# The transposes of w_up's result behind later products, and the first unit's sums of u one stage earlier

## The chip, the cores and the metric

One core of one Trainium2 chip runs the whole kernel. The metric is the device time of one execution in microseconds (us). Three runs of the kernel before took 1495.15, 1499.13 and 1501.15 us; their median, 1499.13 us, stands for it.

## The reference, cut to what matters

One decoder layer on 256 tokens of width 2048: a mixer (state-space heads and attention heads from one projection `w_in`, joined by `w_out`), added to h, and then an MLP, added to h as well. The change lies in the MLP:

```python
def squared_relu_mlp(u, w_up, w_down):
    hdn = jax.nn.relu(jnp.einsum('bsd,df->bsf', u, w_up))
    return jnp.einsum('bsf,fd->bsd', hdn * hdn, w_down)

h = h + rmsnorm(squared_relu_mlp(rmsnorm(h, norm_mlp_pre), w_up, w_down), norm_mlp_post)
```

`w_up` is 2048 x 8192 and `w_down` 8192 x 2048, all in float32.

## The kernel before, in words

**Products.** Every float32 operand is split into a high and a low part of a faster type, `hi` by ScalarE (ACT, L137) and `lo` by VectorE (DVE, L138, which needs `hi`). A product is then three matmuls, lines 249 to 251 (or 331 to 333). Weights come by DMA in tiles `raw` of two slices of 128 rows (a *pair*), 512 columns wide; `raw` has four buffers, `hi` and `lo` five. So ACT's `hi` of a tile waits until TensorE (PE) is done with the tile five before it.

**Units.** `unit` computes two neighbouring blocks of 512 columns at once, for both tiles of 128 tokens, in four accumulators `acc` (PSUM banks). In w_up it has eight pairs. Pairs 2, 4 and 5 are *sevens*: the 2x2x2 block products of such a pair are done with seven multiplications in place of eight, from sums of weight blocks (L212 on DVE) and sums of activation blocks (`sums_of_acts`: L289 to L292 on DVE, then a split into `ha`). Four of the seven products go to four more banks, `more`, which `combine_new` adds in after the last seven. From one unit to the next `acc` and `more` change places. The sums of activations are made in the first unit that needs them and used by all units of that half.

**The end of a w_up unit.** Pairs 6 and 7 come last, first for block 0, then for block 1. When a block's token tile is complete, `up_end` makes a tile `r` or `junk` of it: an add on DVE (L1145) and two activations, relu and square (L1146, L1147). Then `turned` transposes it on PE with four 128x128 transposes (L1156) into the bank that the accumulator had, and splits it into `sh`/`sl` or `ah`/`al`, which are w_down's activations. A unit thus leaves four such *turns*: 1 and 2 for block 0 (token tiles 0 and 1), 3 and 4 for block 1. Their banks are, in the next unit, `more[0]`, `more[2]`, `more[1]` and `more[3]`. There is one buffer `junk` (turns 1 and 3) and there are two buffers `r` (turns 2 and 4, and also the temporary tiles of sums and sevens).

**What sets the order.** Code is recorded in program order, and a scheduler that estimates times then orders each engine's queue; each engine runs its queue in that order. `tc.high_priority` moves an operation ahead of all others that are ready by that estimate; `tc.issue_after(x)` keeps it behind x. Turns are generators in the queue `waiting`: `pump` advances one of them after each pair's products of one block; `drain` runs all to the end, and each unit does that ahead of its first seven. A turn needs two steps: the first does nothing, the second records transposes and splits.

**The stages around the change.** After the mixer and the first rows of w_up, `gemm_features` does one block of w_up with the weights as the stationary operand (L366, L369): the *feature block*. Then come three w_up units (blocks 2 to 7), two w_down units, four w_up units of the second half, and two last w_down units. While the feature block runs, h, which lies in the tiles `ha` and `hb`, goes to DRAM (`copies`, L1134), for the sums of u in the first unit are put in its place. Before the last two units h comes back the same way.

Of the kernel before, what the change touches and what calls it, by code (L numbers as in the profile page):

```python
# [16 lines left out]
P = 128  # L17
S = 256
D = 2048
NT = S // P  # L20
# [28 lines left out]
SUMS = 10  # L49
FINE = 4  # L50
FIRST = 3


def constants():
# [18 lines left out]
def hymba_layer(ctx: ExitStack, tc: tile.TileContext, x, norm_mix_pre, w_in, conv_w, conv_b, dt_bias, a_log,  # L73
                d_skip, ssm_norm_w, w_out, norm_mix_post, norm_mlp_pre, w_up, w_down, norm_mlp_post,
                consts, out):
    nc = tc.nc
    w_in, w_out, w_up, w_down = w_in[0], w_out[0], w_up[0], w_down[0]
# [30 lines left out]
    def part(k):  # L108
        return (sh, sl, k) if k < NK else (att["h"], att["l"], k - NK)
# [3 lines left out]
    ident = cst[:, 0:P]  # L113
# [8 lines left out]
    def bank():  # L122
        return pacc.tile([P, NB], F32, name="acc")

    def psmall():
        return psm.tile([P, NB], F32, name="ps")
# [7 lines left out]
    def split(hi, lo, src, scale=None):  # L134

        if scale is None:
            return (nc.scalar.activation(hi, src, AF.Copy),  # L137
                    nc.vector.tensor_tensor(lo, src, hi.bitcast(F32), op=ALU.subtract))  # L138
        return (nc.scalar.activation(hi, src, AF.Copy, scale=scale),  # L139
                nc.vector.scalar_tensor_tensor(lo, src, scale, hi.bitcast(F32), op0=ALU.mult, op1=ALU.subtract))  # L140
# [21 lines left out]
    def in_place_of_h(acts):  # L162

        a = hp.tile([P, 3 * KB, 2, S], F32R, name="ha")
        room["sums"] = [a[:, k] for k in range(3 * KB)]
        if acts is part:
            b = hp.tile([P, KB, 2, S], F32R, name="hb")
            room["sums"] += [b[:, k] for k in range(KB)]
            room["sums"] += [hp.tile([P, 2, S], F32R, name="wpost", bufs=2) for _ in range(2)]
        else:  # L170
            b = hp.tile([P, NT, NB], F32, name="hb")
            room["shared"] = [[b[:, t] for t in range(NT)],
                              [hp.tile([P, NB], F32, name="wpost", bufs=2) for _ in range(NT)]]
        room["raw"] = None
        room["acts"] = acts
        sums_of.clear()
# [13 lines left out]
    product = {}  # L190
# [39 lines left out]
    waiting = deque()  # L230

    def pump(n=1):
        for _ in range(n):
            if waiting:
                work = waiting.popleft()
                if next(work, work) is not work:
                    waiting.append(work)

    def drain():
        while waiting:  # L240
            pump()
# [11 lines left out]
    def row_tiles(src, c0, ks, acc, acts, first=True, last=True, lag=0, at_end=None, pumps=1, fetch=fetch):  # L253


        held = {}
        n = len(ks)
        for i in range(n + lag):
            if i < n:
                held[i] = weights(src, ks[i] * KB, c0, fetch)  # L260
            for t, at in ((0, i), (1, i - lag)):
                if not 0 <= at < n:
                    continue
                row_tile(acc[t], t, held[at], ks[at], acts, first and at == 0, last and at == n - 1)
                if at == n - 1 and at_end:
                    at_end(t, acc[t])
            pump(pumps)

    def gemm_tokens(src, c0, acts, nk, lag=0, at_end=None, pumps=1):

        acc = [bank() for _ in range(NT)]
        row_tiles(src, c0, range(nk // KB), acc, acts, True, True, lag, at_end, pumps)
        return acc
# [6 lines left out]
    def sums_of_acts(k):  # L280

        if k in sums_of:
            return sums_of[k]
        places = room["sums"][2 * len(sums_of):][:2]
        h_, l_, r = room["acts"](k * KB)
        with tc.high_priority(offset=AHEAD):
            a, c = (tmp().rearrange("p (i s) -> p i s", s=P) for _ in range(2))
            ah_, al_ = (v[:, r:r + KB].bitcast(F32).rearrange("p j (t s) -> p j t s", t=NT) for v in (h_, l_))
            nc.vector.tensor_tensor(a.rearrange("p (j t) s -> p j t s", t=NT), ah_, al_, op=ALU.add)  # L289
            nc.vector.tensor_tensor(c[:, 0:2], a[:, 0::3], a[:, 1:2].to_broadcast([P, 2, P]), op=ALU.subtract)  # L290
            nc.vector.tensor_tensor(c[:, 2], a[:, 0], c[:, 1], op=ALU.add)
            nc.vector.tensor_tensor(c[:, 3], a[:, 2], c[:, 2], op=ALU.subtract)  # L292
            ch, cl = (v.rearrange("p b (t s) -> p (b t) s", t=NT) for v in places)
            split(ch, cl, c)
        sums_of[k] = ch, cl
        return ch, cl
# [38 lines left out]
    def unit(src, n, order, last, acc, more, combine, lag=0, at_end=(None, None), first=True, ending=None):  # L335


        cols = (n * NB, (n + 1) * NB)
        sevens = [k for k, by_seven in order if by_seven]
        for i, (k, by_seven) in enumerate(order):  # L340
            if i + 1 < len(order) and order[i + 1][1]:
                sums_of_acts(order[i + 1][0])
            if by_seven:
                if k == sevens[0]:
                    drain()
                seven(src, *cols, k, acc, more, k == sevens[0], k == sevens[-1])
            else:
                for b in range(2):
                    row_tiles(src, cols[b], [k], acc[b::2], room["acts"], first and i == 0, False,
                              fetch=fetch_next)  # L350
            if k == sevens[-1]:
                combine(more)
        for b in range(2):
            if b and ending:
                ended.append(ending(cols[b], last, acc))
            else:
                row_tiles(src, cols[b], last, acc[b::2], room["acts"], False, True, lag if b else 0, at_end[b],
                          fetch=fetch if b else fetch_next)
# [258 lines left out]
    def first_conv(dst, ft0):  # L617

        for _ in range(FIRST):
            yield  # L620
# [157 lines left out]
    for hb in range(4):  # L778
# [10 lines left out]
        acc = gemm_tokens(w_in, COL_V + hb * NB, act_u, NK)  # L789
# [25 lines left out]
    def tmp():  # L815
        return hp.tile([P, NB], F32, name="r", bufs=2)

    def columns(n):
        return slice(n * NB, (n + 1) * NB)

    def in_mw(n):
        return [[mw[:, t, columns(n + b)] for t in range(NT)] for b in range(2)]
# [197 lines left out]
    acc = [bank() for _ in range(2 * NT)]  # L1020
# [31 lines left out]
    more = [psmall(), bank(), psmall(), bank()]  # L1052
# [7 lines left out]
    def order_of(ks, by_seven):  # L1060
        return [(k, k in by_seven) for k in ks]
# [5 lines left out]
    acc, more = more, acc  # L1067
# [55 lines left out]
    def onto(n):  # L1123

        def at_end(t, acc):
            m = mw[:, t, columns(n)]
            nc.vector.tensor_tensor(m, acc, m, op=ALU.subtract if n % 2 else ALU.add)
        return at_end

    def copies(dst, src):  # L1130

        for t in range(NT):
            for n in range(4):
                nc.scalar.dma_start(dst(t, columns(n)), src(t, columns(n)))  # L1134
                yield

    def in_dram(t, cs):
        return h_d[:, t, cs]
# [12 lines left out]
    def turned(t, k, r, p):  # L1151
        yield
        ts = slice(t * P, (t + 1) * P)
        with tc.high_priority(offset=AHEAD):
            for f in range(4):
                nc.tensor.transpose(p[:, f * P:(f + 1) * P], r[:, f * P:(f + 1) * P], ident)  # L1156
            d_h, d_l, i = part(k)
            split(d_h[:, i:i + 4, ts], d_l[:, i:i + 4, ts], p.rearrange("p (f s) -> p f s", f=4))

    waiting.append(copies(in_dram, of_h))  # L1160
    acc = gemm_features(w_up, NB, begun)
    for b in range(2):
        r = hp.tile([P, 2, S], F32, name="r", bufs=2)
# [3 lines left out]
    drain()  # L1167
    acc, more = [bank() for _ in range(2 * NT)], [psmall(), bank(), psmall(), bank()]
    for hf in range(2):
        in_place_of_h(act_u)  # L1170
        for fb in range(0 if hf else 2, 8, 2):
            unit(w_up[:, hf * 4096:], fb, order_of(range(6), (2, 4, 5)), (6, 7), acc, more,
                 lambda x: combine_new(room["shared"], x), 0, (up_end(fb, 0), up_end(fb + 1, 1)))
            acc, more = more, acc
        if hf == 0:
            drain()
            in_place_of_h(part)
            unit(w_down, 0, order_of(range(14), (4, 6, 9, 11, 13)), (14, 15), acc, more,
                 lambda x: combine_new(in_mw(0), x), 0, (onto(0), onto(1)))
            unit(w_down, 2, order_of((0, 1, 4, 2, 6, 3, 9, 5, 11, 7, 13, 8), (4, 6, 9, 11, 13)), (10, 12, 14, 15), more, acc,  # L1180
                 lambda x: combine_new(in_mw(2), x), 0, (onto(2), onto(3)))
    drain()
    new_h()
    waiting.append(copies(of_h, in_dram))

    def complete(n):
        def at_end(t, acc):
# [41 lines left out]
```

## Time and profile before

| what | us |
|---|---|
| runs (median of three) | 1499.13 |
| the profiled execution's own time | 1494.39 |
| its span, from first to last instruction | 1492.6 |
| PE busy in the span | 1469.8 |
| DVE busy in the span | 1192.9 |
| ACT busy in the span | 847.2 |

Times of single instructions come from the profiled execution, in us from the start of its span; its own time is 1.8 us longer than the span. A matmul of 512 columns is shown as 0.39 us long, but the next one starts 0.23 us after it, since they are pipelined; so a stretch of PE work is measured here from start to start. "Idle before" is the time in which an engine's queue stood still before an instruction, with what released it.

### The profile page before, as it was taken

How to read it: one execution, taken by the hardware profiler on the slowest of the kernel's cores; microseconds unless marked ns; L12 is line 12 of the kernel's file. 1: busy time of each engine (PE TensorE's matmuls, PEld its weight loads, DVE VectorE, ACT ScalarE, POOL GpSimd, SP SyncE). 2: the span in 40 equal slices, each digit the busy share in tenths (PEclk: the TensorE clock that was granted, in tenths of full speed). 3: DMA queues.
4: the chain of work that ended last, by engine and by line, in shares of the span. 5: the costliest groups of instructions: out<-in, count | busy, mean ns of one | idle time of the engine just before them, and what ended most of it. 6: DMA issues, size and time to landing. Idle time of an engine off the chain costs nothing.

```text
span 1492.6 us, 19937 instructions
## 1 busy us (share of the span) xinstructions
PE 1469.8 (98%) x7240; PEld 1235.7 (83%) x7240; DVE 1192.9 (80%) x1764; ACT 847.2 (57%) x1165; POOL 48.7 (3%) x67
## 2 busy tenths in 40 slices
PE   9999999999999999999999999999999999999998
PEld 8888888888888888888878777788888777878886
DVE  6798797886555555588988888889887898889998
ACT  7475675455545454555557566655554665565553
POOL 0003200220000000000000000000000000000000
PEclk9999999999999999999999999999999999999999
DMA  7665666555655555576557466645665666576663
GB/s 268 204 206 177 183 184 193 175 169 169 182 166 175 170 172 180 192 245 204 197 192 228 139 197 192 204 169 192 212 222 176 186 208 197 165 264 211 211 211 113
DMA packets 151283, 287.32 MB, mean 192 GB/s; under 512 B 11680, under 2 KB 14608, under 8 KB 151184
## 3 DMA queue, kind: packets, MB, share of 16 engines
q1 hardware_dynamic: 143456, 272.50, 58.2%
q10 hardware_dynamic: 7728, 13.54, 2.8%
q8 instruction: 57, 0.93, 0.2%
q14 instruction: 42, 0.34, 0.1%
HBM read 281.78 MB, written 4.23 MB: 192 GB/s over the span
## 4 chain that ended last, share of the span: by engine, by line
PE 88%; DVE 5%; ACT 3%; DMA 2%; issue 1%; SPq 0%; POOL 0%; POOLq 0%; ACTq 0%; DVEq 0%
PE acc L366 17%; PE acc L251 12%; PE acc L249 12%; PE acc L250 12%; PE acc L369 8%; PE acc L331 3%; PE acc L332 3%; PE acc L333 3%; PE ps L249 2%; PE ps L250 2%; PE ps L251 2%; DVE lo L138 2%; ACT hi L137 1%; PE ps L333 1%; PE ps L332 1%
## 5 line engine op out<-in xcount | busy, mean ns | idle before, releaser
L138 DVE TENSOR_TENSOR lo<-raw,hi 128x1024 fp32r<-128x1024 f32 (+1 forms) x476 | 580.9, 1224 | 209.8 <-ACT hi L137 203.6
L137 ACT ACTIVATE hi<-raw 128x1024 fp32r<-128x1024 f32 (+1 forms) x476 | 498.7, 1054 | 414.1 <-PE acc L251 131.2
L366 PE MATMUL acc<-ua,hi 128*128 128x512 f32 x680 | 186.9, 404 | 0.5 <-DVE ua L140 0.5
L366 PEld LDWEIGHTS acc<-ua,hi 128*128 128x128 f32 x680 | 120.2, 189 | 19.7 <-DVE ua L140 0.7
L249 PE MATMUL acc<-hi,ua 128*128 128x512 f32 x312 | 122.7, 393 | 0.0
L251 PE MATMUL acc<-hi,ua 128*128 128x512 f32 x312 | 122.2, 392 | 0.0
L250 PE MATMUL acc<-lo,ua 128*128 128x512 f32 x312 | 122.1, 391 | 0.0
L369 PEld LDWEIGHTS acc<-ua,lo 128*128 128x128 f32 x680 | 99.9, 189 | 11.7
L369 PE MATMUL acc<-ua,lo 128*128 128x256 f32 x680 | 103.1, 281 | 0.0
L137 ACT ACTIVATE hi<-e 128x1024 fp32r<-128x1024 f32 x51 | 54.1, 1062 | 61.9 <-DVE e L212 55.9
L249 PE MATMUL acc<-hi,sh 128*128 128x512 f32 x224 | 88.3, 394 | 0.0
L251 PE MATMUL acc<-hi,sl 128*128 128x512 f32 x224 | 87.4, 390 | 0.0
L250 PE MATMUL acc<-lo,sh 128*128 128x512 f32 x224 | 87.3, 390 | 0.0
L366 PE MATMUL acc<-uc,hi 128*128 128x512 f32 x272 | 77.7, 398 | 0.0
L251 PEld LDWEIGHTS acc<-hi,ua 128*128 128x128 f32 x312 | 58.6, 188 | 12.3
L249 PEld LDWEIGHTS acc<-hi,ua 128*128 128x128 f32 x312 | 58.6, 188 | 11.8 <-ACT ua L139 0.3
L250 PEld LDWEIGHTS acc<-lo,ua 128*128 128x128 f32 x312 | 58.7, 188 | 11.7
L250 PE MATMUL acc<-lo,ah 128*128 128x512 f32 x168 | 65.5, 390 | 0.4 <-DVE lo L138 0.4
L251 PE MATMUL acc<-hi,al 128*128 128x512 f32 x168 | 65.4, 389 | 0.0
L249 PE MATMUL acc<-hi,ah 128*128 128x512 f32 x168 | 65.4, 389 | 0.0
L251 PE MATMUL acc<-hi,uc 128*128 128x512 f32 x160 | 62.8, 392 | 0.0
L250 PE MATMUL acc<-lo,uc 128*128 128x512 f32 x160 | 62.6, 392 | 0.0
(442 smaller groups left out, 2941.9 us busy)
## 6 DMA issues: line engine op xcount, KB each, us to landing
raw<-in_w_in_dram SPq DMA_DIRECT2D x190, 512.0 KB, 3.6
raw<-in_w_up_dram SPq DMA_DIRECT2D x128, 512.0 KB, 3.9
raw<-in_w_down_dram SPq DMA_DIRECT2D x110, 512.0 KB, 4.6
raw<-in_w_out_dram SPq DMA_DIRECT2D x46, 512.0 KB, 4.2
uc<-in_w_out_dram SPq DMA_DIRECT2D x18, 512.0 KB, 4.6
uc<-in_w_down_dram SPq DMA_DIRECT2D x18, 512.0 KB, 4.5
bc<-acs_d ACTq DMA_DIRECT2D x8, 512.0 KB, 4.5
xs<-in_x_dram SPq DMA_DIRECT2D x8, 256.0 KB, 6.4
```

Source lines behind the costliest of these rows:

```text
L137: return (nc.scalar.activation(hi, src, AF.Copy), nc.vector.tensor_tensor(lo, src, hi.bitcast(F32), op=ALU.subtract))
L138: nc.vector.tensor_tensor(lo, src, hi.bitcast(F32), op=ALU.subtract))
L249: nc.tensor.matmul(dst, a_h[:, r, ts], hi[:, j], start=begin and j == 0, stop=False)
L250: nc.tensor.matmul(dst, a_h[:, r, ts], lo[:, j], start=False, stop=False)
L251: product[t] = nc.tensor.matmul(dst, a_l[:, r, ts], hi[:, j], start=False, stop=end and j == KB - 1)
L331: nc.tensor.matmul(dst, a_h, hi[:, j], start=own and first, stop=False)
L332: nc.tensor.matmul(dst, a_h, lo[:, j], start=False, stop=False)
L333: nc.tensor.matmul(dst, a_l, hi[:, j], start=False, stop=own and last)
L366: nc.tensor.matmul(acc[f], hi[:, j, f * P:(f + 1) * P], u(k0 + j), start=k0 + j == 0, stop=False, skip_group_check=True)
L369: nc.tensor.matmul(acc[f][:, 0], lo[:, j, f * P:(f + 1) * P], u(k0 + j)[:, 0], start=False, stop=k0 + j == NK - 1, skip_group_check=True)
```

## The change

Three edits, all in the MLP.

1. `turned` puts its transposes behind the last products recorded so far (`issue_after` on both token tiles' products). And the two `drain()` calls behind the w_up units are gone, so that the turns of the last unit of each half go into the w_down unit that follows.
2. The copies of h to DRAM go to the front of `waiting`, four in a step and columns first.
3. `out_of_place` goes on, after the copies, with the sums of u for pairs 2, 4 and 5, so that they are recorded within the feature block; the first unit finds them ready.

```diff
+UP_SEVENS = (2, 4, 5)
...
-    def copies(dst, src):
-
-        for t in range(NT):
-            for n in range(4):
+    def copies(dst, src, step):
+
+        for n in range(4):
+            for t in range(NT):
                 nc.scalar.dma_start(dst(t, columns(n)), src(t, columns(n)))
-                yield
+                if (n * NT + t + 1) % step == 0:
+                    yield
+
+    def out_of_place():
+
+        yield from copies(in_dram, of_h, 4)
+        in_place_of_h(act_u)
+        for k in UP_SEVENS:
+            sums_of_acts(k)
+            yield
...
         with tc.high_priority(offset=AHEAD):
-            for f in range(4):
-                nc.tensor.transpose(p[:, f * P:(f + 1) * P], r[:, f * P:(f + 1) * P], ident)
+            with tc.issue_after(product[0].ins), tc.issue_after(product[1].ins):
+                for f in range(4):
+                    nc.tensor.transpose(p[:, f * P:(f + 1) * P], r[:, f * P:(f + 1) * P], ident)
             d_h, d_l, i = part(k)
             split(d_h[:, i:i + 4, ts], d_l[:, i:i + 4, ts], p.rearrange("p (f s) -> p f s", f=4))
-    waiting.append(copies(in_dram, of_h))
+    waiting.appendleft(out_of_place())
...
     for hf in range(2):
-        in_place_of_h(act_u)
+        if hf:
+            in_place_of_h(act_u)
...
         if hf == 0:
-            drain()
             in_place_of_h(part)
...
-    drain()
     new_h()
-    waiting.append(copies(of_h, in_dram))
+    waiting.append(copies(of_h, in_dram, 1))
```

PE, DVE and ACT have the same instructions before and after; only their order differs. Lines of the changed kernel are higher by 1 up to L1129 and by about 10 behind.

**PE, from the w_up unit of blocks 4 and 5 to the next.** Names carry buffer numbers here; `junk` and `r` are the turns' tiles. Before, turns 1 and 2 stand within the last pair's products of block 1, and turns 3 and 4 within the next unit's first pair:

```order
L250 MATMUL acc_7697<-lo_8415,uc_7192 128x512
L1156 MATMUL ps_7696<-cst_81,junk_8380 128x128 x4
L251 MATMUL acc_7697<-hi_8414,uc_7192 128x512
L1156 MATMUL ps_7698<-cst_81,r_8390 128x128 x4
L249 MATMUL acc_7697<-hi_8414,uc_7192 128x512
```

```order
L249 MATMUL acc_7693<-hi_8470,ua_7190 128x512
L1156 MATMUL acc_7697<-cst_81,junk_8424 128x128 x4
L250 MATMUL acc_7693<-lo_8471,ua_7190 128x512
L1156 MATMUL acc_7699<-cst_81,r_8434 128x128 x4
L251 MATMUL acc_7693<-hi_8470,ua_7190 128x512
```

Now turn 1 stands behind the unit's last product (ten products further on) and turn 2 behind pair 0 of block 0. Turns 3 and 4 are interleaved in one run behind pair 1, the last pair ahead of the first seven; this is that run's last transpose with the start of the seven:

```order
L1167 MATMUL acc_7727<-cst_81,r_8434 128x128
L332 MATMUL ps_7724<-hi_8542,ua_7190 128x512
L333 MATMUL ps_7724<-lo_8543,ua_7190 128x512
L334 MATMUL ps_7724<-hi_8542,ua_7190 128x512
L332 MATMUL acc_7720<-hi_8542,ua_7190 128x512
L333 MATMUL acc_7720<-lo_8543,ua_7190 128x512
L334 MATMUL acc_7720<-hi_8542,ua_7190 128x512
L332 MATMUL ps_7726<-hi_8548,ha_7608 128x512
L333 MATMUL ps_7726<-lo_8549,ha_7608 128x512
L334 MATMUL ps_7726<-hi_8548,ha_7608 128x512
L332 MATMUL acc_7721<-hi_8552,ha_7608 128x512
L332 MATMUL acc_7725<-hi_8548,ha_7608 128x512
```

Turn 3's bank, acc_7725, is written again by the eleventh product behind the run, so its splits have ten products' time; turn 4's bank comes three products later. The transposes have moved from in front of the place where their data are made to the place where their banks are wanted. The same holds for the other four passages from one w_up unit to the next.

**DVE, from the last w_up unit to w_down.** `al` are the low parts of the turns; `lo_11797` is the low part of the first seven's second weight tile. Before, all turns are split ahead of pair 2:

```order
L138 TENSOR_TENSOR al_3668<-acc_7693,ah_3667 128x4x128
L138 TENSOR_TENSOR al_3668<-acc_7695,ah_3667 128x4x128
L138 TENSOR_TENSOR lo_11746<-uc_11655,hi_11745 128x1024
L292 TENSOR_TENSOR r_11737<-r_11736,r_11737 128x128
L138 TENSOR_TENSOR lo_11764<-uc_11655,hi_11763 128x1024
L138 TENSOR_TENSOR ua_11653<-r_11737,ua_11653 128x512
L212 TENSOR_TENSOR e_11786<-raw_11782,raw_11784 128x512
L212 TENSOR_TENSOR e_11786<-e_11786,raw_11784 128x512
L138 TENSOR_TENSOR lo_11791<-raw_11782,hi_11790 128x1024
L212 TENSOR_TENSOR r_11787<-e_11786,raw_11782 128x512
L212 TENSOR_TENSOR raw_11784<-raw_11784 128x512
L138 TENSOR_TENSOR lo_11797<-e_11786,hi_11796 128x1024
```

Now, behind `lo_11791`:

```order
L139 TENSOR_TENSOR al_3668<-acc_7721,ah_3667 128x4x128
L291 TENSOR_TENSOR r_11722<-r_11721 128x256
L292 TENSOR_TENSOR r_11722<-r_11721,r_11722 128x128
L139 TENSOR_TENSOR al_3668<-acc_7723,ah_3667 128x4x128
L293 TENSOR_TENSOR r_11722<-r_11721,r_11722 128x128
L213 TENSOR_TENSOR r_11787<-e_11786,raw_11782 128x512
L213 TENSOR_TENSOR raw_11784<-raw_11784 128x512
L139 TENSOR_TENSOR ua_11635<-r_11722,ua_11635 128x512
L139 TENSOR_TENSOR lo_11797<-e_11786,hi_11796 128x1024
```

The second split belongs to turn 4, whose transposes stand on PE directly ahead of the first seven (pair 3), and the tile r_11722 of the sums takes turn 4's own buffer. Eight operations from there on stand ahead of a low part that this seven needs.

**DVE, feature block and first w_up unit.** Before, the sums of u stand in the first unit, among the weights of its sevens:

```order
L138 TENSOR_TENSOR sl_80<-r_7681,sh_79 128x512
L289 TENSOR_TENSOR r_7740<-ua_7190 128x512
L290 TENSOR_TENSOR r_7741<-r_7740 128x256
L291 TENSOR_TENSOR r_7741<-r_7740,r_7741 128x128
L292 TENSOR_TENSOR r_7741<-r_7740,r_7741 128x128
L212 TENSOR_TENSOR r_7789<-e_7788,raw_7784 128x512
L212 TENSOR_TENSOR raw_7786<-raw_7786 128x512
L138 TENSOR_TENSOR ha_7700<-r_7741,ha_7700 128x512
```

Now they stand among the weights of the feature block, and only sevens' work is left in the unit:

```order
L139 TENSOR_TENSOR lo_7731<-raw_7728,hi_7730 128x1024
L139 TENSOR_TENSOR ha_7608<-r_7613,ha_7608 128x512
L290 TENSOR_TENSOR r_7642<-ua_7190 128x512
L139 TENSOR_TENSOR sl_80<-ps_7553,sh_79 128x4x128
L291 TENSOR_TENSOR r_7643<-r_7642 128x256
L139 TENSOR_TENSOR lo_7749<-raw_7746,hi_7748 128x1024
L292 TENSOR_TENSOR r_7643<-r_7642,r_7643 128x128
```

On ACT the eight copies of h to DRAM stand between the same activations before and after, all of them ahead of the feature block.

2 lines of the change are left out of this document (1 added, 1 removed).

## The prediction

> **What bounds the kernel now.** I read the page's first part, the waits of PE, PE's timeline around each wait, and then DVE and ACT there.
>
> ```profile
> span 1492.6 us, 19937 instructions
> PE 1469.8 (98%) x7240; PEld 1235.7 (83%) x7240; DVE 1192.9 (80%) x1764; ACT 847.2 (57%) x1165; POOL 48.7 (3%) x67
> ...
> PE acc L1156 <- ACT junk L1147: 6.2, 4, 2.7
> PE ps L1156 <- ACT junk L1147: 3.8, 3, 1.4
> ```
>
> PE stands still for only 22.8 us of the span (1492.6 - 1469.8), and nothing in the change takes work off PE. So all that can be won is what PE waits for. Of that, 10.0 us are seven waits of the transposes (L1156) for the square of their tile (L1147). The timeline of PE has them one by one, with three more waits in the first w_up unit (L331):
>
> ```profile
> 852.98 0.73 PE L331 MATMUL acc<-hi,ha 128*128 128x512 f32 x2 [1.13 <-ACT hi L137]
> 857.72 0.50 PE L331 MATMUL acc<-hi,ha 128*128 128x512 f32 x1 [0.98 <-ACT hi L137]
> 860.31 0.50 PE L331 MATMUL acc<-hi,ha 128*128 128x512 f32 x1 [0.94 <-ACT hi L137]
> ...
> 878.03 0.39 PE L249 MATMUL acc<-hi,ua 128*128 128x512 f32 x1
> 879.13 0.66 PE L1156 MATMUL acc<-cst,junk 128*128 128x128 f32 x4 [0.71 <-ACT junk L1147]
> ...
> 879.85 0.60 PE L1156 MATMUL acc<-cst,r 128*128 128x128 f32 x4
> 880.21 0.48 PE L251 MATMUL acc<-hi,ua 128*128 128x512 f32 x1
> 880.52 0.39 PE L249 MATMUL acc<-hi,ua 128*128 128x512 f32 x1
> 880.75 0.40 PE L250 MATMUL acc<-lo,ua 128*128 128x512 f32 x1
> ...
> 917.91 0.66 PE L1156 MATMUL ps<-cst,junk 128*128 128x128 f32 x4 [1.39 <-ACT junk L1147]
> 963.32 0.66 PE L1156 MATMUL acc<-cst,junk 128*128 128x128 f32 x4 [1.69 <-ACT junk L1147]
> 1175.83 0.66 PE L1156 MATMUL ps<-cst,junk 128*128 128x128 f32 x4 [0.98 <-ACT junk L1147]
> 1220.53 0.66 PE L1156 MATMUL acc<-cst,junk 128*128 128x128 f32 x4 [1.03 <-ACT junk L1147]
> 1265.70 0.65 PE L1156 MATMUL ps<-cst,junk 128*128 128x128 f32 x4 [1.43 <-ACT junk L1147]
> 1311.73 0.66 PE L1156 MATMUL acc<-cst,junk 128*128 128x128 f32 x4 [2.73 <-ACT junk L1147]
> ```
>
> Products start 0.23 us apart (880.52, 880.75). From 878.03 to 879.13 pass 1.10 us, so that wait costs 0.87, which is 0.16 more than its idle column: the matmul before is shown 0.39 long but would have had a successor after 0.23. With 0.16 on each of ten waits, the seven of the transposes cost 9.96 + 1.12 = 11.1 us and the three of the first unit 3.05 + 0.48 = 3.5. Gross, 14.6 us are at stake, 1.0% of the span.
>
> **The transposes, first place.** Turn 1 moves ten products back, or 2.27 us, in five of the six passages where it waits. The dearest wait there is 1.69 + 0.16 = 1.85 us, so its tile is ready when PE comes, with 0.4 us to spare; DVE also makes `junk` one low part earlier than before. Turn 3, which waited at 879.13, moves 10 us back. These seven rows but the last go to zero: -8.2 us (11.1 less 2.9).
>
> In the last passage (1311.73) turn 1 moves twelve products, 2.7 us, against a wait of 2.9; and ACT's new order has a weight tile's `hi` (1.06, below) between relu and square where a shorter relu stood. I take 0.6 us of waiting; bounds 0 (the `hi` could run earlier) and 1.5 (its DMA may land late).
>
> **The transposes, second place.** What can be late next is the bank. Turns 3 and 4 now stand right ahead of the seven that writes their banks, and ACT and DVE have to empty them in between. For the first passage:
>
> ```profile
> 888.03 0.39 PE L331 MATMUL acc<-hi,ua 128*128 128x512 f32 x1
> ...
> 879.82 0.60 ACT L137 ACTIVATE sh<-acc 128x512 fp32r<-128x512 f32 x1 [0.22 <-PE acc L1156]
> 888.23 1.06 ACT L137 ACTIVATE hi<-raw 128x1024 fp32r<-128x1024 f32 x1 [2.09 <-PE acc L251]
> ...
> 876.23 0.68 DVE L138 TENSOR_TENSOR sl<-acc,sh 128x512 fp32r<-128x512 f32 x1
> 889.32 2.59 DVE L138 TENSOR_TENSOR lo<-raw,hi 128x1024 fp32r<-128x1024 f32 x2 [2.46 <-ACT hi L137]
> ...
> 903.60 1.23 DVE L138 TENSOR_TENSOR lo<-raw,hi 128x1024 fp32r<-128x1024 f32 x1
> 905.93 0.39 PE L332 MATMUL acc<-lo,ha 128*128 128x512 f32 x1
> ```
>
> The seven starts at 888.03; ACT's next `hi` starts at 888.23, when PE gives its buffer back, and its `lo` runs from 889.32 to 890.55. In the new order the eight transposes come in at 888.03. Four cost 0.36 us (879.85 to 880.21) and 0.08 more at the next product, so eight cost 0.9 and the seven starts at 888.95. Behind that `hi` ACT takes turn 3's high part (889.3 to 889.9) and turn 4's (to 890.4); behind that `lo` DVE takes turn 3's low part (890.5 to 891.15) and turn 4's (to 891.75). PE wants turn 3's bank after ten products, at 888.95 + 2.27 = 891.2, and turn 4's at 891.9. Both are free just in time. I take 0.2 us a passage, 1.0 for five; bounds 0, and 1.2 each if one more low part (1.23) gets ahead.
>
> The split pair also delays DVE's later weights by 1.3 us, while PE is 0.9 later itself. The tightest is the second weight block of the third seven, ready at 903.60 + 1.23 = 904.83 and wanted at 905.93: of 1.1 us, 0.7 stay. No term.
>
> **The passage to the last w_down units.** Here turn 4's transposes stand directly ahead of the first seven too, but DVE has its split, and everything that waits for it, ahead of that seven's low parts. From the start of turn 4's transposes: they end at 0.6; two adds of the sums (0.42, 0.29) follow, since their tile takes turn 4's buffer; the split (0.68), the third add (0.29), two sums of weights (0.69 each), the sums' low part (0.68) and `lo` of the seven's second tile (1.23). Rows for these are the ones of the first unit, next fence. Less 0.07 to 0.09 of overlap each, that `lo` is done at about 5.3 us. PE's new order starts five products early on high parts alone and reaches that `lo` after 0.45 of transposes and eleven products, 2.95 us. Cost: 2.4 us; behind it the other low parts come as PE wants them. Bounds 1 and 3.5. That DVE stands behind transposes even before is in this row:
>
> ```profile
> 1319.09 0.43 DVE L290 TENSOR_TENSOR r<-r 128x256 f32<-128x256 f32 x1 [0.42 <-PE acc L1156]
> ```
>
> [...]
>
> In the middle passage (from blocks 6 and 7 of the first half to w_down) the first seven is pair 4, and turn 4 is done a pair and a half, or 8 us, ahead of it: the 5.3 us chain fits. No term.
>
> **Sums of u.**
>
> ```profile
> 803.70:828.80 25.10, 25.10 (x148) 22.02 (x147) 17.95 (x26) 13.43 (x20) 0.54 (x1) 1.00 0.75 232
> ...
> 843.00:863.40 20.40, 17.35 (x75) 13.24 (x74) 19.94 (x29) 11.25 (x14) 0.00 (x0) 1.00 0.55 157
> ...
> L212 DVE TENSOR_TENSOR r<-e,raw 128x512 f32<-128x512 f32 x3 | 2.1, 690 | 0.1
> L138 DVE TENSOR_TENSOR ha<-r,ha 128x512 fp32r<-128x512 f32 x3 | 2.0, 682 | 0.0
> L289 DVE TENSOR_TENSOR r<-ua 128x512 f32<-128x512 f32 x2 | 1.4, 682 | 0.0
> L290 DVE TENSOR_TENSOR r<-r 128x256 f32<-128x256 f32 x3 | 1.3, 418 | 0.0
> L291 DVE TENSOR_TENSOR r<-r 128x128 f32<-128x128 f32 x3 | 0.9, 289 | 0.1
> L292 DVE TENSOR_TENSOR r<-r 128x128 f32<-128x128 f32 x3 | 0.9, 289 | 0.1
> ...
> 822.43 1.06 ACT L137 ACTIVATE hi<-raw 128x1024 fp32r<-128x1024 f32 x1 [1.68 <-PE acc L366]
> 825.22 1.06 ACT L137 ACTIVATE hi<-raw 128x1024 fp32r<-128x1024 f32 x1 [1.73 <-PE acc L366]
> ```
>
> In the first two rows the columns after the length are PE, PEld, DVE and ACT. In the first unit's sevens DVE is busy 19.94 of 20.40 us, and PE waits for it through ACT. One set of sums is 0.68 + 0.42 + 0.29 + 0.29 + 0.68 = 2.36 us, three are 7.1. The waits sum to 3.5, so with 7.1 taken off they go: -3.5. In the feature block DVE is idle 25.10 - 17.95 = 7.15 us, which the 7.1 fill. What hides that is the lead: ACT's `hi` there waits for PE to give buffers back, every 2.8 us (822.43, 825.22), so weights are four tiles or 11 us ahead of PE. Without that lead DVE could be late by what does not fit, some 1 us. I take 0.
>
> **The copies of h.**
>
> ```profile
> L1134 ACTq DMA_DIRECT2D h_d<-hb x2: 326/326/326, 791.8 to 794.4; - x2
> ...
> DMA to landing us min/median/max: 2.0/5.3/7.1
> ```
>
> The scheduler already issues the last one at 794.4, it lands by 801.5 (794.4 + 7.1), and the feature block, where the sums now write that place, comes later still. The same slots on ACT hold them in the new order. 0 us.
>
> **Sum.** -8.2 - 2.9 + 0.6 (turn 1) + 1.0 (banks) + 2.4 (last passage) - 3.5 (sums) = -10.6 us on an execution of 1494.39 us (span 1492.6 and 1.8 around it): 1483.8, or 0.71% less. That execution is 0.3% under the median of the runs; the same share of 1499.13 gives 1488.5 us.
>
> **Rivals.** *The banks come late (0.18).* One more low part ahead of turn 3's split in each of five passages costs 1.2 instead of 0.2. For it: the margin above is under 0.1 us. Against: it is the scheduler's order, and DVE was idle 2.46 us before 889.32. Gain 10.6 - 5.0 = 5.6: 1493.5, no change.
>
> *The first unit's waits stay (0.10).* For it: its four weight sums and four low parts of a seven fill DVE without the sums, and the feature block hands it a full queue. Against: later units have the same sevens without such waits. Gain 7.1: 1492.0, at the edge of no change.
>
> *DVE held in every passage (0.06), slower.* What I find at the last passage, DVE standing at turn 4's split with a seven's weights behind it, happens at the five passages from one w_up unit to the next if DVE gets there before PE. Price 2.4 each, and, as only 0.7 us are spare at the third seven, 1.7 more there. It decides from (14.6 - 3.0) / 5 = 2.3 us a passage; at 4.1 it is 20.5 + 3.0 - 14.6 = 8.9 slower: 1508. For it: the row at 1319.09. Against: the new order has the first seven's low parts ahead of those splits.
>
> *The change does not do what it says (0.03):* turn 1 waits at its new place as long as at its old. Then the tiles' chain would have to move back 2.27 us as well; gain 3 at most, 1496.
>
> **How the numbers follow.** The forecast has 0.63. A measurement here tells about 0.5%, 7.5 us, from no change. The forecast's 10.6 is over that by 3; with its bounds (14.6 down to 6) some 0.57 of its 0.63 count as faster, half of the second rival's 0.10, and 0.03 of the first's: 0.65. Slower is the third rival's 0.06 with nothing else; the rest, 0.29, is no change. The low end is everything won (14.6: 1484.5) less 3 us of spread, as the three runs show it; the high end is the first two rivals plus the same spread. 1482 to 1497.
>
> **What would show it.** PE's waits have no row of the transposes over 0.3 us except near 1311; no L331 row in the first unit; a new wait of L332 or L333 of 2 to 3 us at the first seven of the last w_down pair of units; DVE nearly without idle time in the feature block; the copies to DRAM at 777 to 794 as before. The forecast is wrong if waits appear at L331 after each run of eight transposes, or if DVE idles for `PE acc` of the transposes with weights behind it.

## The result, and the profile after

The changed kernel takes 1482.28 us (median of four runs, 1481.80 to 1484.99), the kernel before, run beside it, 1498.69 us (four runs, 1495.15 to 1501.15). The ratio is 0.9896, with an interval of 0.9873 to 0.9919: 16.4 us less, where 10.6 were forecast. The time lies 6 us under the forecast and just inside the low end of its range. Measured a second time, beside the last experiments below, the gain was 13.9 us.

The page of the changed kernel starts like this:

```profile
span 1483.2 us, 19920 instructions
PE 1470.9 (99%) x7240; PEld 1237.3 (83%) x7240; DVE 1190.9 (80%) x1764; ACT 848.6 (57%) x1165; POOL 48.7 (3%) x67
```

PE has the same 7240 matmuls and is as busy as before (1470.9 against 1469.8), so it stands still for 12.3 us where it stood still for 22.8. The span is 9.4 us shorter. The waits of PE in the MLP that are left (engine, line, releaser: total, times, longest):

```profile
PE acc L332 <- ACT hi L138: 1.0, 1, 1.0
...
PE acc L332 <- ACT ua L138: 0.9, 1, 0.9
PE ps L251 <- DVE lo L139: 0.6, 1, 0.6
...
PE acc L1167 <- ACT junk L1157: 0.5, 1, 0.5
```

Of the seven waits of the transposes (10.0 us) one of 0.5 is left, and the three of the first unit (3.0 us) are gone: L332 is L331 of before, but its two rows stand elsewhere. All four rows lie in the last passage, as PE's timeline of the changed kernel shows (start, duration, then what it waited for):

```profile
1299.63 0.66 PE L1167 MATMUL acc<-cst,junk 128*128 128x128 f32 x4 [0.49 <-ACT junk L1157]
...
1312.54 0.50 PE L251 MATMUL ps<-lo,sh 128*128 128x512 f32 x1 [0.60 <-DVE lo L139]
...
1318.40 0.60 PE L1167 MATMUL acc<-cst,r 128*128 128x128 f32 x4
...
1319.99 0.40 PE L334 MATMUL ps<-hi,sl 128*128 128x512 f32 x1
1321.30 0.73 PE L332 MATMUL acc<-hi,ua 128*128 128x512 f32 x2 [0.91 <-ACT ua L138]
1323.06 0.85 PE L332 MATMUL acc<-hi,ua 128*128 128x512 f32 x2 [1.02 <-ACT hi L138]
...
1324.17 0.63 PE L333 MATMUL acc<-lo,ua 128*128 128x512 f32 x1
1324.60 0.63 PE L334 MATMUL acc<-hi,ua 128*128 128x512 f32 x1
...
1327.06 0.39 PE L333 MATMUL acc<-lo,ua 128*128 128x512 f32 x1
```

Turn 1 waits 0.49 + 0.16 = 0.65 us (1299.63) and a product of the third pair 0.76 (1312.54). Turn 4's transposes are at 1318.40, and the first seven behind them waits twice: from 1319.99 to 1321.30 for the high part of the sums (`ua`), which costs 1.08, and to 1323.06 for a high part of weights, 1.19. Together that is 2.27 us, where the forecast had 2.4. Then come rows of a kind that before's profile has nowhere in its MLP: from 1323.7 to 1326.9 the products are 0.63 us long and start 0.43 apart instead of 0.23. The windows of the changed kernel show why (columns: length, busy time of PE, PEld, DVE, ACT and POOL, granted clock of PE, DMA share, GB/s):

```profile
803.20:828.30 25.10, 25.10 (x146) 21.90 (x145) 23.43 (x38) 15.08 (x22) 0.54 (x1) 1.00 0.75 231
842.50:862.90 20.40, 20.40 (x92) 16.89 (x91) 20.07 (x25) 12.12 (x14) 0.00 (x0) 1.00 0.68 194
...
1323.50:1326.90 3.40, 3.40 (x10) 2.67 (x9) 3.40 (x5) 2.65 (x4) 0.00 (x0) 0.50 0.49 155
```

In the third window the granted clock is 0.50, and the clock record of that trace has it so for 3.41 us. Eight products that start 0.2 us later each cost about 1.6 us. The first two windows answer those of the prediction. In the feature block DVE is now busy 23.43 of 25.10 us (17.95 before) and PE still all of the time. In the first unit PE is busy 20.40 of 20.40 (17.35 before).

### The profile page after: what moved, and what is told of

Its sections match the earlier page's. It is cut to its first block, busy times and chain, and to the rows that moved or that the text cites. A ratio compares the mean times of both kernels' runs of the same rounds, so it can differ in the third digit from the quotient of the medians.

```text
span 1483.2 us, 19920 instructions
## 1 busy us (share of the span) xinstructions
PE 1470.9 (99%) x7240; PEld 1237.3 (83%) x7240; DVE 1190.9 (80%) x1764; ACT 848.6 (57%) x1165; POOL 48.7 (3%) x67
## 4 chain that ended last, share of the span: by engine, by line
PE 94%; DVE 2%; DMA 1%; issue 1%; ACT 1%; SPq 0%; POOL 0%; POOLq 0%; ACTq 0%; DVEq 0%
PE acc L367 17%; PE acc L250 13%; PE acc L251 13%; PE acc L252 13%; PE acc L370 9%; PE acc L333 4%; PE acc L334 4%; PE acc L332 4%; PE ps L251 3%; PE ps L252 3%; PE ps L250 3%; PE ps L332 1%; PE ps L334 1%; PE ps L333 1%; DVE lo L139 1%; PE ps L701 1%
## 5 line engine op out<-in xcount | busy, mean ns | idle before, releaser
L252 PE MATMUL acc<-hi,uc 128*128 128x512 f32 x160 | 62.3, 389 | 0.0
L250 PE MATMUL acc<-hi,uc 128*128 128x512 f32 x160 | 62.2, 389 | 0.0
```

What stands on the lines that cost most here:

```text
L250: nc.tensor.matmul(dst, a_h[:, r, ts], hi[:, j], start=begin and j == 0, stop=False)
L252: product[t] = nc.tensor.matmul(dst, a_l[:, r, ts], hi[:, j], start=False, stop=end and j == KB - 1)
```

## The experiments

What had to be told apart is which edit brings which part, what the last passage really waits for, and why the kernel gained more by its runs (16.4) than by its profiled executions (9.4). In the expectations the first theory (W where it has a letter) is the forecast's: the gain is the waits of PE that the trace shows, edit by edit, and nothing else. The rival on the surplus (C) is the clock: a wait costs more than its length where a stretch of half clock follows it.

**The kernel before once more**, without an edit, to see how its profile differs from one execution to the next.

> The kernel before once more, for a second profile of it and for the scatter of its time. Theory W (waits alone): the change won 9.4 us in the profiled spans (1492.6 to 1483.2), and the 16.4 us between the medians are scatter; this run's ratio is 1.000 within 0.2%, its profile has the same ten waits of PE (14.6 us) and a granted clock of full speed up to the end. Rival C (clock): in many executions of the kernel before the granted clock falls to half for 3.4 us behind some of its ten waits, each time at a cost of 1.7 us, as the profile of the changed kernel shows it once, at 1323.5 us; then this profile has one to four such stretches, and its span is 2 to 7 us above 1492.6.

Measured: 1497.75 us (12 runs, 1495.71 to 1500.97), ratio 1.0004 (0.9994 to 1.0015). Its profiled execution has a span of 1495.5 us, 2.9 more than the first one's, and one stretch of half clock, as the rival C has it. The waits are at the same places but not of the same length, and one of them is followed by half clock. PE's timeline of that run, and two windows of it:

```profile
964.82 0.66 PE L1156 MATMUL acc<-cst,junk 128*128 128x128 f32 x4 [2.05 <-ACT junk L1147]
...
966.28 0.63 PE L250 MATMUL acc<-lo,uc 128*128 128x512 f32 x1
966.71 0.63 PE L251 MATMUL acc<-hi,uc 128*128 128x512 f32 x1
```

```profile
962.70:966.10 3.40, 1.35 (x11) 1.21 (x11) 1.54 (x2) 3.40 (x6) 0.00 (x0) 1.00 0.97 307
966.20:969.50 3.30, 3.30 (x9) 2.53 (x8) 2.42 (x3) 0.99 (x3) 0.00 (x0) 0.50 0.68 227
```

So the kernel before has such stretches too, and the profile that the prediction was made from happened to have none. How often, the mean granted clock tells that is listed with each run. Of the 25 runs of the kernel before beside this experiment:

| mean granted clock | runs | mean time, us |
|---|---|---|
| 0.999 | 3 | 1494.85 |
| 0.998 | 7 | 1496.51 |
| 0.997 | 10 | 1498.27 |
| 0.996 | 4 | 1499.42 |
| 0.995 | 1 | 1499.56 |

From 0.999 to 0.996 the time rises by 4.6 us, or 1.5 us for each 0.001, which is 0.001 of the span. One stretch of 3.41 us at half clock takes 3.41 x 0.5 / 1495 = 0.0011 off the mean, so 0.997, the commonest value, is one or two stretches more than 0.999, as an estimate. (The clock is halved at the program's end as well, for 2.6 to 6.1 us of the span in the ten profiles. With 6.1 us, in the changed kernel's profile, PE has only two products there, 2.07 us of its busy time; with 4.3, in before's, the same two came ahead of it and took 1.13. So this part costs 0.9 us or less, as an estimate, but its length differs by as much as one stretch takes off the mean, and so blurs the table.)

**Edit 1 alone**: the transposes behind the last products, no drains; copies and sums of u as before.

```diff
+            with tc.issue_after(product[0].ins), tc.issue_after(product[1].ins):
                 for f in range(4):
...
-            drain()
             in_place_of_h(part)
...
-    drain()
     new_h()
```

> Edit 1 alone: issue_after and no drains; copies and sums as before. Theory W: the seven waits at the transposes go (11.1 us) and the last passage gives back what it does in the changed kernel (0.65 + 0.76 + 2.27 of waits and 1.7 of clock, 5.4), so 5.7 us won, ratio 0.996; the three waits of the first w_up unit (3.5 us) stay. Rival S (the sums do it): the transposes' waits only move, as DVE stands behind the turns; less than 2 us won, ratio above 0.9985. Rival C adds up to 5 us to the win, ratio 0.993.

Measured: 1488.97 us (6 runs, 1488.46 to 1491.86), against 1497.80 beside it; ratio 0.9946 (0.9931 to 0.9961). The spans of the profiled executions differ by 6.0 us (1492.6 to 1486.6), close to the 5.7 of theory W; the medians differ by 8.8, between W and rival C. PE's timeline of that run:

```profile
852.56 0.73 PE L331 MATMUL acc<-hi,ha 128*128 128x512 f32 x2 [1.13 <-ACT hi L137]
857.30 0.50 PE L331 MATMUL acc<-hi,ha 128*128 128x512 f32 x1 [0.97 <-ACT hi L137]
859.90 0.50 PE L331 MATMUL acc<-hi,ha 128*128 128x512 f32 x1 [0.94 <-ACT hi L137]
...
1016.51 0.50 PE L250 MATMUL ps<-lo,ah 128*128 128x512 f32 x1 [0.76 <-DVE lo L138]
...
1324.98 0.73 PE L331 MATMUL acc<-hi,ua 128*128 128x512 f32 x2 [0.91 <-ACT ua L137]
1326.73 1.22 PE L331 MATMUL acc<-hi,ua 128*128 128x512 f32 x2 [1.02 <-ACT hi L137]
```

The first unit waits to 0.01 us as before, and no transposes wait. The price at the last first seven is there to the digit, with the half clock behind it; a wait of 0.92 (0.76 + 0.16) inside the first w_down unit (1016.51) has no like in the two profiles of the changed kernel. The waits of the turns and that of the sevens are thus edit 1's alone.

**Edits 2 and 3 alone**: copies first, sums of u in the feature block; the turns as before.

```diff
+        in_place_of_h(act_u)
+        for k in UP_SEVENS:
+            sums_of_acts(k)
+            yield
...
-    waiting.append(copies(in_dram, of_h))
+    waiting.appendleft(out_of_place())
...
-    waiting.append(copies(of_h, in_dram))
+    waiting.append(copies(of_h, in_dram, 1))
```

> Edits 2 and 3 alone: copies first and sums of u in the feature block; turns and drains as before. Theory W: the three waits of the first unit go, 3.5 us, ratio 0.9977; the seven at the transposes stay at 11.1 us, and no wait appears in the feature block. Rival L (the lead is too short): the feature block gets waits of its own, and the win is below 2 us. Rival S: 8 us or more, ratio below 0.995.

Measured: 1493.29 us (8 runs, 1491.19 to 1497.02), ratio 0.9972 (0.9959 to 0.9985): 4.5 us less by the medians, for 3.5 forecast. Its waits of PE have no row of the first unit any more, and the transposes wait as they did:

```profile
PE acc L1166 <- ACT junk L1157: 6.9, 4, 2.0
PE ps L1166 <- ACT junk L1157: 3.7, 3, 1.9
```

Behind one of them, at 1309.26 with 2.03 us, there is again a stretch of half clock. 8.8 for edit 1 and 4.5 for the others make 13.3 us; both together gave 16.4 and, the second time, 13.9 (below). Within these intervals, about 2 us to either side or more, the edits add up; a smaller effect of one on the other would not be seen.

**Edit 2 alone**: the copies ahead in the queue, four in a step.

```diff
-        for t in range(NT):
-            for n in range(4):
+        for n in range(4):
+            for t in range(NT):
                 nc.scalar.dma_start(dst(t, columns(n)), src(t, columns(n)))
-                yield
+                if (n * NT + t + 1) % step == 0:
+                    yield
...
-    waiting.append(copies(in_dram, of_h))
+    waiting.appendleft(out_of_place())
```

> Edit 2 alone: the copies of h to DRAM first in the queue, four in a step, columns first; sums in the first unit as before. Theory W: the copies keep their slots on ACT, issued from 777 to 794 us, all ten waits stay, ratio 1.000 within 0.2%. Rival D (the copies held the sums back): the first unit's three waits shrink by more than 1 us.

Measured: 1496.62 us (12 runs, 1495.55 to 1499.91), ratio 0.9995 (0.9985 to 1.0005): no change that these runs can show. The copies keep their slots on ACT (777.9 to 795.2 us), and the waits are those of before:

```profile
PE acc L1162 <- ACT junk L1153: 6.7, 4, 3.1
PE ps L1162 <- ACT junk L1153: 3.3, 3, 1.4
PE acc L332 <- ACT hi L138: 3.1, 3, 1.1
```

**The changed kernel once more**, with the next three on one chip, where the kernel before took 1497.09 us (7 runs, 1495.58 to 1498.59).

> The changed kernel once more, beside the next three on one chip. Theory W: ratio 0.990 to 0.994; waits at the last passage alone (0.65, 0.76 and 2.27 us). Whether the granted clock falls to half behind the 2.27 us again: if it follows from the wait alone, yes, for 3.4 us at about 1323; if it depends on where the wait lies in a window that runs on its own, in some profiles and not in others.

Measured: 1483.21 us (4 runs, 1483.09 to 1484.76), ratio 0.9910 (0.9896 to 0.9925), 13.9 us less than before. PE's timeline of that run has the pair of waits at the first seven unchanged:

```profile
1321.44 0.73 PE L332 MATMUL acc<-hi,ua 128*128 128x512 f32 x2 [0.91 <-ACT ua L138]
1323.19 1.20 PE L332 MATMUL acc<-hi,ua 128*128 128x512 f32 x2 [1.02 <-ACT hi L138]
```

The half clock behind it is there again, at 1323.3. The waits of 0.65 and 0.76 us at turn 1 and in the third pair are not: these differ from one execution to the other, the pair at the seven does not.

**The drains put back**, the rest of the change kept: the turns of the last unit of each half are done between the units again.

```diff
         if hf == 0:
+            drain()
             in_place_of_h(part)
...
+    drain()
     new_h()
```

> The changed kernel with both drains put back: turns behind the last products, but those of a half's last unit all recorded ahead of w_down. Theory W: the wait at the first seven of the last w_down units (2.27 us) goes, and with it the half clock (1.7 us), since turn 4 is split two pairs earlier; in return PE waits at the two passages to w_down for the squares of turns 3 and 4, 0.5 to 1.5 us each. Net within 2 us of the changed kernel. Rival P (a drain lets the turns stand in PE's way): 3 us or more for each of the two passages, so 2 to 4 us slower than the changed kernel.

Measured: 1484.81 us (4 runs, 1484.11 to 1485.74), ratio 0.9919 (0.9904 to 0.9934), 1.6 us more than the changed kernel beside it. Its timeline of PE:

```profile
961.14 0.66 PE L1167 MATMUL acc<-cst,r 128*128 128x128 f32 x4 [0.70 <-ACT r L1157]
...
1301.34 0.33 PE L1167 MATMUL acc<-cst,r 128*128 128x128 f32 x1 [0.94 <-ACT r L1157]
...
1306.04 0.55 PE L1167 MATMUL acc<-cst,r 128*128 128x128 f32 x3 [0.98 <-ACT r L1157]
...
1326.10 0.50 PE L250 MATMUL ps<-hi,sh 128*128 128x512 f32 x1 [0.40 <-ACT hi L138]
1327.36 0.51 PE L251 MATMUL ps<-lo,sh 128*128 128x512 f32 x1 [0.76 <-DVE lo L139]
```

The 2.27 us at the first seven are gone, and the half clock with them, but the turns wait again, 0.86 + 1.10 + 1.14 us (with 0.16 on each row) at the two passages into w_down, and 0.56 + 0.92 us follow at the products behind the seven. At the last passage the turns thus cost 2.24 us, more than the 0.5 to 1.5 expected. By the trace, 2.27 us of waiting with a stretch at half clock, 1.6, stand in place of 4.6 us of other waits. That leaving the drains out pays is likely, not shown: the runs of the two kernels overlap, and the profiled span with the drains is even 0.6 us shorter (1482.3 against 1482.9).

**The first seven of the last two w_down units one pair later**, all else as changed. If what PE waits for at 1321.3 and 1323.1 is the chain behind turn 4, one pair more of products covers it; if it were a late transfer, it would move along.

```diff
-    unit(w_down[4096:], 0, order_of(range(14), (3, 6, 8, 11, 13)), (14, 15), acc, more,
+    unit(w_down[4096:], 0, order_of(range(14), (4, 6, 8, 11, 13)), (14, 15), acc, more,
...
-    unit(w_down[4096:], 2, order_of((0, 1, 3, 2, 6, 4, 8, 5, 11, 7, 13, 9), (3, 6, 8, 11, 13, 9)), (10, 12, 14, 15), more, acc,
+    unit(w_down[4096:], 2, order_of((0, 1, 4, 2, 6, 3, 8, 5, 11, 7, 13, 9), (4, 6, 8, 11, 13, 9)), (10, 12, 14, 15), more, acc,
```

> The changed kernel with the first seven of both last w_down units at pair 4 in place of pair 3, as in the first half's w_down units. Theory W: turn 4 is then done 8 us ahead of that seven and the chain behind it (5.3 us) fits: the 2.27 us and the half clock behind them go, 3 to 4 us won against the changed kernel; the 0.65 and the 0.76 stay. Rival F (the weights' DMA is what is late there, not the turn): the wait moves to pair 4 and less than 1 us is won.

Measured: 1481.10 us (4 runs, 1480.71 to 1481.52), ratio 0.9895 (0.9878 to 0.9911). All that PE waits for in the last passage is now this:

```profile
1299.72 0.66 PE L1167 MATMUL acc<-cst,junk 128*128 128x128 f32 x4 [0.26 <-ACT junk L1157]
...
1312.59 0.50 PE L251 MATMUL ps<-lo,sh 128*128 128x512 f32 x1 [0.56 <-DVE lo L139]
```

The 2.27 us and the half clock are gone: it was turn 4's chain. The kernel is 2.1 us faster than the changed one beside it, and no run of the one reaches a run of the other; by its median it is the fastest of all that were run. By the spans of the profiled executions the difference is 4.0 us (1482.9 to 1478.9), about 2.27 + 1.6; by the runs it is only the wait. So either the half clock does not come in every execution of the changed kernel, or it comes elsewhere in the other: the mean clocks of the runs (0.998 in three of four, and in all four) don't decide that for the runs with 0.998. A run with 0.999 has room for at most 4.4 us of half clock, and a stretch with the shortest end of a profile takes 3.4 + 2.6 = 6.0. So by this estimate the fourth run here, and three of the first four, had no stretch.

**The same, and h comes back later**: the copies of h from DRAM are recorded behind the first of the last two units. As changed, ACT issues them from 1287.6 to 1312.3, around both waits that are left.

```diff
     new_h()
-    waiting.append(copies(of_h, in_dram, 1))
...
+    waiting.append(copies(of_h, in_dram, 1))
```

> As later_seven, and the copies of h back from DRAM only behind the first of the two last w_down units. Theory W: the 0.76 us at pair 2 of the first of these units, where DVE waits for a weight tile's DMA, are due to the copies on the same DMA engines and go; 0.5 to 1 us won against later_seven. Rival F: that tile is late because its place, the tile uc, comes free only at the end of the w_up unit; then the 0.76 stay.

Measured: 1482.25 us (4 runs, 1480.46 to 1483.12), ratio 0.9900 (0.9885 to 0.9915): 1.2 us more than without it, by runs that overlap. Its timeline of PE, and its copies of h (columns: count, shortest, median and longest in ns, first and last start):

```profile
1300.85 0.66 PE L1167 MATMUL acc<-cst,junk 128*128 128x128 f32 x4 [0.96 <-ACT junk L1157]
```

```profile
L1135 ACTq DMA_DIRECT2D ha<-h_d x6: 326/326/383, 1288.4 to 1301.5; - x6
...
L1135 ACTq DMA_DIRECT2D hb<-h_d x2: 456/456/457, 1301.9 to 1313.4; - x2
```

The copies did not move: the scheduler put them between the same activations as before, from 1288.4 to 1313.4 here and from 1287.9 to 1312.4 in the run without this edit. What moved on PE are turns 3 and 4, each twelve products forward (turn 3 to 1312.74 from 1315.23). So this run says nothing about the copies, and whether they made the third pair's low part late stays open. That turn 1 waits longer than in the run before (0.96 against 0.26) happens ahead of all that moved on PE, and whether that comes from this edit or differs from one execution to the next is not known.

## Why the prediction was right, and where it was off

The time fell inside the range for a reason that the working doesn't give. It had 14.6 us at stake in all, and the first measurement has 16.4; only the 3 us of spread below that sum held it. That part was luck. The terms, one by one:

**The transposes, first place (-8.2): right.** No profile with edit 1 and without drains has a wait of a transpose outside the last passage. **Turn 1 in the last passage (-2.9 + 0.6): right within its bounds.** It cost 0.65 us in one profile of the changed kernel and nothing in the other.

**The banks (+1.0): mis-sized, about half.** DVE and ACT did as forecast. In the first passage the eight transposes start at 881.91, and DVE splits both turns here:

```profile
883.20 1.23 DVE L139 TENSOR_TENSOR lo<-raw,hi 128x1024 fp32r<-128x1024 f32 x1 [2.04 <-ACT hi L138]
884.34 1.28 DVE L139 TENSOR_TENSOR sl<-acc,sh 128x512 fp32r<-128x512 f32 x2
```

The second split ends at 885.62, 3.7 us behind the start of the transposes; the forecast had 891.75 - 888.03, the same 3.7. PE reaches turn 3's bank with the second of these two products:

```profile
884.85 0.73 PE L332 MATMUL acc<-hi,ha 128*128 128x512 f32 x2
885.42 0.40 PE L333 MATMUL acc<-lo,ha 128*128 128x512 f32 x1
```

The two take 0.57 us from start to start instead of 0.46. The same 0.1 us stands at this product in all five passages, and the kernel before, where the product behind it follows after 0.23 us, has none; so the banks cost 0.5 to 0.6 us in all. "Just in time" was late by a tenth; the 0.2 us a passage were a margin that the working itself did not give. The first rival (one more low part ahead of the split) did not come: one low part stands there, as in the sum.

**The last w_down units (+2.4): right in size and place, wrong in the link.** The chain was counted up to the low part of the second weight tile (`lo<-e`). That count is right: it ends at 1323.65, 5.25 us behind the start of turn 4's transposes, where 5.3 were forecast. But when PE came to it, at 1324.17, it was done. What PE had waited for came earlier in the same chain: ACT's high part of the sums (`ua`) and of a weight tile. DVE's timeline of the changed kernel, and ACT's:

```profile
1319.03 0.43 DVE L291 TENSOR_TENSOR r<-r 128x256 f32<-128x256 f32 x1 [1.60 <-PE acc L1167]
...
1319.70 0.68 DVE L139 TENSOR_TENSOR al<-acc,ah 128x512 fp32r<-128x512 f32 x1
1320.30 0.28 DVE L293 TENSOR_TENSOR r<-r 128x128 f32<-128x128 f32 x1
1320.62 0.69 DVE L213 TENSOR_TENSOR r<-e,raw 128x512 f32<-128x512 f32 x1
1321.23 0.68 DVE L213 TENSOR_TENSOR raw<-raw 128x512 f32<-128x512 f32 x1
...
1322.43 1.22 DVE L139 TENSOR_TENSOR lo<-e,hi 128x1024 fp32r<-128x1024 f32 x1
```

```profile
1320.62 0.63 ACT L138 ACTIVATE ua<-r 128x512 fp32r<-128x512 f32 x1 [0.98 <-DVE r L293]
1321.94 1.06 ACT L138 ACTIVATE hi<-raw 128x1024 fp32r<-128x1024 f32 x1 [0.70 <-DVE raw L213]
```

DVE stands 1.60 us at the add that needs turn 4's buffer back from PE, with weights of the seven queued behind it; ACT's `ua` waits 0.98 for the third add and `hi` 0.70 for the sum of weights. ACT's `hi` ends at 1323.00 and the low part 0.65 us later, and PE has three products between the two, 0.7 us at full clock. That the two ends lie so close is why the size came out. The working does not give that, so the closeness (2.27 for 2.4) is in part luck. The stretch of half clock behind it, 1.6 us, had no term. A chain over two engines has to be followed on both: the forecast let ACT's steps hide. The 2.4 also took for granted that DVE does not go past an add that waits. No run tests that alone; what they show is DVE's row of 1.60 us, with the sums of weights (L213) started behind it, at 1320.62, and PE's 2.27 us. Putting the seven a pair later took the whole term away, as the forecast argued for the middle passage: it then starts at 1324.38, 5.9 us behind the start of turn 4's transposes (1318.45), and the chain fits.

**The first unit's sums (-3.5): right.** The waits are gone, in the changed kernel and with edits 2 and 3 alone, and the feature block took the sums: PE has no idle time there, and DVE has 5.5 us more work (23.43 against 17.95) in that window, of the 7.1 forecast. **The copies (0): right.** Moving them alone gave 0.9995.

**None of the rivals came.** DVE was held by a transpose at one passage only, the forecast's own.

**The conversion to the median: wrong, and it is most of the 6 us.** The sum was -10.6 on an execution of 1494.39 us, and the forecast took "the same share" of the median. Two things were off. First, the small terms: without turn 1, and with the banks at the 0.5 that they cost, the sum is -11.7. Second, the granted clock. The profiled execution of before has a mean clock of 0.999, that of the changed kernel 0.997. The three other runs of the changed kernel have 0.999 and 1482.12 us on average. Against 1494.39 at the same clock the gain is 12.3 us, and beside the second measurement of the changed kernel the two runs with 0.999, one of each kernel, give 1495.58 - 1483.09 = 12.5: both within 0.8 us of that sum. The remaining 4 of 16.4 us is the way from 1494.39 to the median of before, 1498.69, for the execution that was profiled had no stretch of half clock ahead of its end, and most runs of that kernel, by the estimate under the table above, have one or two. Part of the 4 us is also the sampling of four runs, since the second measurement gave 13.9 in place of 16.4. The changed kernel may have fewer such stretches: the mean clock is 0.9984 over its eight runs, and 0.9973 and 0.9979 over the 25 and the 7 runs of before beside the experiments. As the end of the program is in these means too, that is not shown.

That the waits which were removed are what set off the half clock in before is likely, not shown either. For it: all five stretches in the ten profiles (apart from the start and the end of the program) stand directly behind waits of 2.2 to 2.3 us, two of them behind a transpose's wait that edit 1 removes, three behind the pair at the seven that it adds. The longest waits of all, 2.73 and 3.05 us by their rows in the profiles of before and of edit 2 alone, have none behind them. In the clock records of the traces the time from one change of the clock to the next, up to the half clock at the program's end, is a whole number of 3.4133 us: 1481.38 us are 434 of them in before; in the changed kernel 1317.55 are 386, the stretch of 3.413 is one, and the 150.19 behind it are 44; 959.15 are 281 in the second profile of before. Laid out in steps of this length, the wait of 2.73 us lies across a boundary at 1310.82. The windows on both sides of it:

```profile
1307.41:1310.82 3.41, 1.59 (x8) 0.97 (x6) 3.25 (x4) 1.95 (x3) 0.00 (x0) 1.00 0.99 374
1310.82:1314.24 3.42, 2.51 (x15) 2.21 (x16) 1.43 (x2) 3.42 (x7) 0.00 (x0) 1.00 0.98 337
```

PE is busy 1.59 and 2.51 us there, and 1.71 and 2.06 around the boundary in the wait of 3.05. In the five windows that end where a stretch begins PE is busy 1.37 to 1.49 us, and 1.74 with edit 1 alone. That a wait of some 2 us is followed by half clock or not by where it falls in such a step is the author's guess from these numbers; no run shows it. No limit on the busy time explains them either, as 1.74, with a stretch behind it, lies above 1.59, without one. Edit 1 alone, without waits of transposes, has a mean clock of 0.9975 over six runs, like before; it has the pair at the seven, with a stretch behind it in its profile, so that does not speak against the waits as the cause.

## What to carry to other kernels

Where one engine is busy 98% of the span, what a reordering can win is the list of that engine's waits, start to start, with the half clock that may follow them (here 1.6 to 1.7 us for waits of 2.2 to 2.3), and each wait can be followed to its new place; here the three large terms held, and the two small ones stayed within their bounds. Set up the sum against an execution, and look at the granted clock of that execution and of the other runs before carrying it to a median: the profile without a stretch of half clock was not the median run here (1494.39 against 1498.69). And look in the new trace whether an edit moved what it was meant to move: the last one here did not. Where a wait is moved to the next consumer, give that consumer a pair more of distance: the last 2 us here were in the place of one seven.

## What the runs showed of the hardware

In five profiles TensorE's clock was halved for one stretch behind waits that cost PE 2.2 to 2.3 us. In the changed kernel's the clock record gives the stretch 3.413 us. The two windows of the kernel before above show the same: 1.35 us busy of 3.40, then clock 0.50. During a stretch products of 512 columns start 0.43 us apart instead of 0.23, so it costs 1.6 to 1.7 us, nearly as much as the wait that precedes it.

A gap of 2.05 us had a stretch behind it (second profile of before), and so had gaps of 0.91 and 1.02 us with two products between (changed kernel, twice, and edit 1 alone); gaps of 2.73 us (before) and 3.05 us (edit 2 alone) had none. So the length of a gap does not tell it. The changes of the clock in the records lie a whole number of 3.4133 us apart, and the waits of 2.73 and 3.05 us lie across a boundary of such steps (above). Whether that is why they had none is not shown: no run here moves one wait to and fro within a step, which would be the test.
